# One row-scale step for the last row block, K-tile order in the first up group, and another stage order in a 2048 x 1024 decoder block

## Chip, cores and metric

The kernel runs on one core of a Trainium2 chip. The metric is device time in microseconds (us), the median of several executions; less is better. Before the change it is 2471.93 us (three runs, 2469.47 to 2472.9).

## What is computed

One decoder block on x, 2048 rows (S) by 1024 columns (D), everything in float32:

```
n  = rms_norm(x, w1)
m  = concat(gated_deltanet(n), retention(n))     # 4 heads of 128 each
h  = x + m @ w_out                               # 1024 x 1024
n2 = h * rsqrt(mean(h*h, -1) + 1e-6) * w2        # the second norm
u  = causal_dwconv3(n2 @ w_up)                   # two halves: gate and value
y  = rms_norm(h + (silu(u_gate) * u_value) @ w_down, w3)
```

The mixers (gated deltanet and retention) work in chunks with a state that is carried from chunk to chunk. The up projection makes 2 x 2816 columns.

## The kernel before, in words

**Arithmetic.** Each fp32 product is three TensorE (PE) matmuls: both operands are split into a rounded part (hi) and a rest (lo), and hi·hi, hi·lo, lo·hi are added in one bank of PSUM (mm3, lines 118 to 120). The split itself is two instructions: ACT copies the hi part (line 1045 for the output projection, 1101 for up's x and weights), and DVE subtracts it to get the lo part (1046, 1102). On top of that the three large projections (w_out, up, down) use a scheme of seven products in place of eight: seven sums of sub-blocks are formed on DVE (lines 1121 for x, 1151 for weights), then split, then multiplied, and the seven results are added up with the right signs (1017 for w_out, 1183 for up).

**Stages.** The rows are four blocks of 512 (b = 0 to 3). A string, ORDER (line 46), names the stages of all blocks in the order in which the program is written: 2b0 is the first base stage of block 2, 3W5 product 5 of block 3's output projection, 3N its second norm. The base stages (`gdn_base`) solve the triangular systems of the deltanet on POOL, as a long chain of small instructions (lines 771 and 773). A scheduler then places the instructions of the neighbouring stages on each engine, and the numbers of buffers in BUFS bound how far ahead it may go. After the mixers of all blocks follow `mlp_up` (22 column groups, each for two halves q of the rows) and `mlp_down`.

**The second norm (W_items).** When the last product of a row tile t has been added, `done(t)` stores the tile (hd), squares and sums it on ACT (1029), forms mean plus eps on DVE (1030, 128x1), takes the power -0.5 on POOL (1031, 128x1) and scales the tile in place on ACT (1032, 128x1024, tile Cw). Each block has four tiles. `norm2` then transposes the scaled tiles on PE (line 1080, bank nps) and writes them to DRAM (n2d), from where `mlp_up` reads them as xr.

**The border between mixers and up.** Half q = 0 of up needs blocks 0 and 1 only, so the first up groups run while block 3's output projection (products W1, W2, W6, W7, W5, W4, W3) ends. Four steps prepare them: `load_w` fetches a group's weights into wur, forms their sums and splits them (tile wu); `prep_x` does the same to the rows (xr, sums st, tiles x, for kt = 0 to 3). Their DMAs stand in SyncE's queue (SP) behind fences, given as FW (first weights) and F0 to F3 (the rows of kt = 0 to 3): each is an index, counted from the end, in the list of weight loads of block 3's output projection. `group(q, g, ...)` multiplies. Two groups, those in `outer`, run K-tile by K-tile over seven banks at once; all others run one product after another, each over its four K-tiles, with the bank of p1 used again for product 2 and that of p5 for product 3 (lines 1202 to 1211; ACT copies p1 out on 1203 and 1205).

Of the kernel before, what the change touches and what calls it, by code (L numbers as in the profile page):

```python
# [10 lines left out]
AF = mybir.ActivationFunctionType  # L11
ALU = mybir.AluOpType
# [12 lines left out]
NACC = 6  # L25
NWU = 9
NWV = 5
FW = -6
F0 = -7
F1 = -2  # L30
F2 = -1
F3 = -3
NU = 3
NPB = 7
NPM = 4
# [3 lines left out]
NXR = 7  # L39
FD = 4  # L40
NFRESH = 2
BUFS = {"n1": 8, "ykq": 14, "kv": 6, "NT": 13, "AT": 6, "o": 9, "n2s": 21, "xk": 2, "og": 4, "co": 7, 
        "Cw": 10, "wx": 1, "wsq": 6, "pr": 2, "pt": 3, "pv": 2, "ca": 8, "D": 9, "rk": 13, "rq": 9, 
        "rv": 25, "Ar": 4, "xs": 4, "sx": 4, "Cb": 9, "Nb": 14, "rot": 1, "rrow": 1}

ORDER = ("0pro 0v0 0k0 0dec 0a0 0q0 0a1 0a3 0a2 0h1 0b0 0h0 0L0 0Q0 0r00 0b1 0Q1 0r01 0r02 0kq 0r03 0L1 0h3 "
# [7 lines left out]
P = 128  # L54
S = 2048
D = 1024
KT = D // P
TB = 512
NB = S // TB
NT = TB // P  # L60
# [3 lines left out]
NP = NF // 2  # L64
EPS = 1e-6
# [8 lines left out]
def unit(pool, tag, shape, dt=F32, **kw):  # L74

    n = int(np.prod(shape[1:]))
    t = pool.tile([P, U1], dt, tag=tag, name=tag, **kw)[:, :n]
    if len(shape) == 3:
        t = t.rearrange("p (a b) -> p a b", a=shape[1])
    elif len(shape) == 4:  # L80
        t = t.rearrange("p (a b c) -> p a b c", a=shape[1], b=shape[2])
    return t
# [93 lines left out]
def prep_v(tc, pool, marks, w, k, nm, kept, drp, caps):  # L176

    nc = tc.nc
    POOL = nc.gpsimd
    r = [unit(pool, "pr", [P, 2, TB], bufs=caps[0]) for j in range(2)]  # L180
    for j in range(2):
        chained(tc, marks, r[j].rearrange("p a n -> p (a n)"), w[k, :, 2 * j * TB:2 * (j + 1) * TB])
    q = [r[j // 2][:, j % 2] for j in range(4)]
    tt = [unit(pool, "pt", [P, 2, TB], bufs=caps[1]) for j in range(2)]
    t1, t2, t3, t4 = (tt[j // 2][:, j % 2] for j in range(4))
    for d, a, b_ in ((t1, q[1], q[0]), (t3, q[3], q[1]), (t2, q[3], t1), (t4, q[2], t2)):
        POOL.tensor_tensor(d, a, b_, op=ALU.subtract)
    for i, src in ((1, q[0]), (2, q[2]), (3, q[3]), (5, t1), (7, t3), (6, t2), (4, t4)):
        v = split_v(nc, unit(pool, "pv", [P, 2, TB], F32R, bufs=caps[2]), src)
        kept[i, k] = drp.tile([P, 2, TB], F32, name=f"{nm}{i}_{k}", tag=f"{nm}{i}_{k}", bufs=1)  # L190
        nc.sync.dma_start(kept[i, k], v.bitcast(F32))
# [52 lines left out]
def mixers(ctx, tc, base, base_used, marks, drp, mm3, gamma, mhalf, n1w, n2w, gcw, gv127, epsr, gnw, n2d, hd,  # L244
           x, xT, w_kq, w_v, w_g, w_i, w_rk, w_r0, w_r, w_o, rows, masks, rot):
    nc = tc.nc
    PE, ACT, DVE, POOL = nc.tensor, nc.scalar, nc.vector, nc.gpsimd
# [96 lines left out]
    def kept_v(kept, i, k):  # L344
        v = unit(ap_, "wv", [P, 2, TB], F32R, bufs=NWV)
        chained(tc, marks, v.bitcast(F32), kept[i, k])
        return v

    def prep(k, which):
        def f(_):  # L350
            w, nm, kept = ((w_i, "wi", wic), (w_o, "wo", wvc))[which]
            prep_v(tc, ap_, marks, w, k, nm, kept, drp, (BUFS["pr"], BUFS["pt"], BUFS["pv"]))
        return f
# [12 lines left out]
    def al(tag, shape, dt=F32):  # L366
        return unit(ap_, tag, shape, dt, **({"bufs": BUFS[tag]} if tag in BUFS else {}))

# [6 lines left out]
    def bank(nm):  # L375
        return psb.tile([P, 512], F32, tag="bk", name=nm)

    def mbank(nm):
        return psm.tile([P, 512], F32, tag="mx", name=nm)
# [7 lines left out]
    def small(nm, n=16, bufs=2):  # L387
        if nm not in ring:
            ring[nm] = [pc(bufs, n), 0, bufs]
        e = ring[nm]  # L390
        e[1] += 1
        return e[0][:, e[1] % e[2]]
# [621 lines left out]
    def W_items(b):  # L1014
        C = {}
        ss = small("hss", 16)
        add = lambda o, a, b_: DVE.tensor_tensor(o, a, b_, op=ALU.add)

        def addx(c, src, t, dh):
            xr = al("wx", [P, TB])  # L1020
            r0 = b * TB + t * P
            marks["x", b, t, dh] = nc.sync.dma_start(xr, x[r0:r0 + P, dh * TB:(dh + 1) * TB])
            add(c, src, xr)

        def done(t):
            c = C[t]
            nc.sync.dma_start(hd[b][t * P:(t + 1) * P, :], c)
            sq = al("wsq", [P, D])
            ACT.activation(sq, c, AF.Square, accum_out=ss[:, t:t + 1])
            DVE.tensor_scalar(ss[:, t:t + 1], ss[:, t:t + 1], 1.0 / D, EPS, op0=ALU.mult, op1=ALU.add)  # L1030
            POOL.tensor_tensor(ss[:, 8 + t:9 + t], ss[:, t:t + 1], mhalf[:, :1], op=ALU.pow)
            ACT.activation(c, c, AF.Copy, scale=ss[:, 8 + t:9 + t])

        def product(i):
            def f(_):
                vs = [kept_v(wvc, i, k) for k in range(NH)]
                if b == NB - 1:
                    marks.setdefault("wo", marks["wl"][-16:]).extend(marks["vl"][-NH:])
                for m in range(2):
                    if i == 1:  # L1040
                        for t in (m, 2 + m):
                            C[t] = al("Cw", [P, D])
                    r = sts[b]["co"][i][:, :, m * P:(m + 1) * P]
                    u = unit(ap_, "wu2", [P, 2, NH, P], F32R, bufs=NU)
                    ACT.activation(u[:, 0], r, AF.Copy)
                    DVE.tensor_tensor(u[:, 1], r, u[:, 0].bitcast(F32), op=ALU.subtract)
                    ps = bank("wo")
                    mm3(ps, [(u[:, 0, k], u[:, 1, k], vs[k][:, 0], vs[k][:, 1]) for k in range(NH)])
                    c11, c12 = C[m][:, :TB], C[m][:, TB:]
                    c21, c22 = C[2 + m][:, :TB], C[2 + m][:, TB:]  # L1050
                    if i == 1:
                        ACT.activation(c12, ps, AF.Copy)
                        addx(c11, ps, m, 0)
                    elif i == 2:
                        add(c11, ps, c11)
                    elif i == 6:
                        add(c12, ps, c12)
                    elif i == 7:
                        add(c21, ps, c12)
                    elif i == 5:  # L1060
                        add(c22, ps, c21)
                        add(c12, ps, c12)
                        for c, t, dh in ((c21, 2 + m, 0), (c22, 2 + m, 1), (c12, m, 1)):
                            addx(c, c, t, dh)
                    elif i == 3:
                        add(c12, ps, c12)
                        done(m)
                    else:
                        add(c21, ps, c21)
                        done(2 + m)  # L1070
            return f

        def norm2(_):
            for kk in range(4):
                ns = al("n2s", [P, 2, TB])
                for i in range(2):
                    k = 2 * kk + i
                    ps = mbank("nps")
                    for m in range(NT):
                        PE.transpose(ps[:, m * P:(m + 1) * P], C[m][:, k * P:(k + 1) * P], ident)  # L1080
                    ACT.activation(ns[:, i], ps, AF.Copy, scale=n2w[:, k:k + 1])
                marks["n", b, kk] = nc.scalar.dma_start(n2d[b, kk].rearrange("k p t -> p k t"), ns)
        return {f"W{i}": [(None, None, product(i))] for i in ORD_DN} | {"N": [(None, None, norm2)]}

    sts = [dict() for _ in range(NB)]
    items = {b: A_items(b, sts[b]) | W_items(b) for b in range(NB)}
    items["load"], items["parts"] = load_chunk, load_parts
    return items
# [3 lines left out]
def mlp_up(ctx, tc, marks, drp, mm3, mcw, mhalo, n2d, wud, aud, w_u):  # L1092
    nc = tc.nc
    PE, ACT, DVE, POOL = nc.tensor, nc.scalar, nc.vector, nc.gpsimd
# [159 lines left out]

    gs = [(0, g) for g in range(2 * NP)]
    gs += [(1, g) for g in (*range(NFRESH, NP + 1), *range(NFRESH), *range(NP + 1, 2 * NP))]
    outer = [gs[2 * NP - 1], gs[2 * NP]]
    marks["f1"] = [g // 2 for q, g in gs[2 * NP::2]]
    st = {}
    fence = [marks["wo"][j].ins for j in (FW, F0, F1, F2, F3)]  # L1260
    with tc.issue_after(fence[0]):
# [209 lines left out]
```

## Time and profile before

| | us |
|---|---|
| median of three runs | 2471.93 |
| the profiled execution, its time | 2470.93 |
| its span, first to last instruction | 2469.1 |
| PE busy | 2408.9 |
| DVE busy | 1642.7 |
| ACT busy | 1010.1 |
| POOL busy | 549.2 |
| mean granted PE clock (of 1) | 0.994 |

The span is made of mixers up to about 1166 us, the border up to about 1221 us, up, and down to the end. In the profile's rows, L118 is line 118 of the kernel, PE and PEld are matmuls and weight loads of TensorE, PEclk is the clock that TensorE was granted; in a timeline each row has start, duration, engine, line, output<-input, and in brackets the idle time ahead of it and what ended it; in the waits, the total, the count and the longest.

### The profile page before, as it was taken

What the parts mean: (1) busy time and instruction counts of PE and PEld (TensorE: products, weight loads), DVE (VectorE), ACT (ScalarE), POOL (GpSimd) and SP (SyncE); (2) the same over time, 40 slices, a digit from 0 to 9 for tenths busy, and PEclk for the clock granted to TensorE, in tenths of its full rate; (3) what the DMA queues carried; (4) which work ended last, traced back from release to release, by engine and by line L of the source; (5) the groups of instructions that cost most, each with busy time, mean ns of one, the idle gap of its engine ahead of it and who ended that gap; (6) DMA issues with size and microseconds to landing.
All of it is one profiled execution on the core that took longest, in us unless ns stands there. A gap on an engine that the chain in (4) does not pass through costs nothing.

```text
span 2469.1 us, 35787 instructions
## 1 busy us (share of the span) xinstructions
PE 2408.9 (98%) x12508; PEld 2022.4 (82%) x12508; DVE 1642.7 (67%) x3260; ACT 1010.1 (41%) x2125; POOL 549.2 (22%) x865
## 2 busy tenths in 40 slices
PE   9999899999999999999899999999999999999998
PEld 7877788888888888787588888888888888888887
DVE  5886966355754646436989889896575567555673
ACT  5554634444522543325554344442232225333341
POOL 1385214701083104530211000000000001422030
PEclk9999999999999999999999999999999999999999
DMA  5887866674565565546698788787646879864782
GB/s 214 289 302 273 311 226 229 237 246 167 203 235 189 193 231 187 195 177 233 220 337 301 288 312 294 282 298 248 226 155 245 284 242 285 265 211 141 237 257 95
DMA packets 281572, 590.05 MB, mean 239 GB/s; under 512 B 40560, under 2 KB 120880, under 8 KB 281392
## 3 DMA queue, kind: packets, MB, share of 16 engines
q1 hardware_dynamic: 264528, 573.40, 66.2%
q10 hardware_dynamic: 16864, 14.37, 1.8%
q8 instruction: 98, 1.61, 0.3%
q14 instruction: 82, 0.67, 0.1%
HBM read 395.42 MB, written 192.25 MB: 238 GB/s over the span
## 4 chain that ended last, share of the span: by engine, by line
PE 81%; POOL 8%; DVE 4%; DMA 3%; issue 2%; ACT 1%; SPq 0%; ACTq 0%; POOLq 0%; DVEq 0%
PE p L118 11%; PE p L120 11%; PE p L119 11%; PE d L120 6%; PE d L119 6%; PE d L118 6%; PE tok L561 4%; PE tok L563 4%; PE tok L562 4%; POOL pers L773 3%; POOL pers L771 3%; PE chm L118 2%; PE chm L119 2%; PE chm L120 2%; PE wo L120 1%
## 5 line engine op out<-in xcount | busy, mean ns | idle before, releaser
L119 PE MATMUL p<-x,wu 128*128 128x512 f32 x1176 | 459.3, 391 | 3.3 <-DVE x L1102 3.3
L118 PE MATMUL p<-x,wu 128*128 128x512 f32 x1176 | 454.6, 391 | 7.1 <-ACT x L1101 6.7
L120 PE MATMUL p<-x,wu 128*128 128x512 f32 x1176 | 452.3, 390 | 0.0
L561 PE MATMUL tok<-wc,n 128*128 128x512 f32 (+2 forms) x768 | 277.7, 364 | 5.8 <-ACT n L449 5.5
L562 PE MATMUL tok<-wc,n 128*128 128x512 f32 (+2 forms) x768 | 276.4, 361 | 0.0
L563 PE MATMUL tok<-wc,n 128*128 128x512 f32 (+2 forms) x768 | 275.3, 362 | 0.0
L118 PEld LDWEIGHTS p<-x,wu 128*128 128x128 f32 x1176 | 221.0, 188 | 56.9 <-ACT x L1101 8.7
L119 PEld LDWEIGHTS p<-x,wu 128*128 128x128 f32 x1176 | 221.4, 188 | 51.4 <-DVE x L1102 6.2
L120 PEld LDWEIGHTS p<-x,wu 128*128 128x128 f32 x1176 | 221.4, 188 | 46.0 <-DVE wu L1102 0.2
L1225 DVE SCALAR_TENSOR_TENSOR acc<-uc,base,acc 128x1022 f32<-128x1022 f32 (+1 forms) x176 | 221.0, 1279 | 39.0 <-ACT acc L1222 38.9
L1183 DVE TENSOR_TENSOR uc<-p,uc 128x512 f32<-128x512 f32 x224 | 153.4, 688 | 122.5 <-PE p L120 122.0
L118 PE MATMUL d<-v,uu 128*128 128x512 f32 x448 | 174.3, 389 | 0.0
L119 PE MATMUL d<-v,uu 128*128 128x512 f32 x448 | 174.3, 389 | 0.0
L120 PE MATMUL d<-v,uu 128*128 128x512 f32 x448 | 174.3, 389 | 0.0
L561 PEld LDWEIGHTS tok<-wc,n 128*128 128x128 f32 x768 | 146.8, 191 | 26.4 <-ACT n L449 5.5
L220 POOL TENSOR_TENSOR vt<-vr 128x512 f32<-128x512 f32 x33 | 51.6, 1574 | 516.5 <-DVE acc L1238 421.7
L563 PEld LDWEIGHTS tok<-wc,n 128*128 128x128 f32 x768 | 146.7, 191 | 20.0
L562 PEld LDWEIGHTS tok<-wc,n 128*128 128x128 f32 x768 | 146.8, 191 | 19.3
L119 PE MATMUL chm<-n,wc 128*128 128x512 f32 x384 | 151.2, 394 | 0.0
L120 PE MATMUL chm<-n,wc 128*128 128x512 f32 x384 | 151.2, 394 | 0.0
L118 PE MATMUL chm<-n,wc 128*128 128x512 f32 x384 | 151.1, 393 | 0.0
L771 POOL TENSOR_TENSOR pers<-Nb,pers 128x248 f32<-128x248 f32 (+30 forms) x248 | 119.5, 482 | 69.5 <-DMA Nb<-z 53.5
(256 smaller groups left out, 4804.8 us busy)
## 6 DMA issues: line engine op xcount, KB each, us to landing
wu<-wu SPq DMA_DIRECT2D x280, 512.0 KB, 5.9
wc<-wd SPq DMA_DIRECT2D x166, 512.0 KB, 5.6
wv<-wo SPq DMA_DIRECT2D x112, 512.0 KB, 6.4
wd<-wc SPq DMA_DIRECT2D x60, 512.0 KB, 4.9
ur<-au SPq DMA_DIRECT2D x56, 512.0 KB, 5.0
wur<-in_w_u SPq DMA_DIRECT2D x48, 512.0 KB, 6.3
au<-st SPq DMA_DIRECT2D x88, 256.0 KB, 4.1
vr<-in_w_d SPq DMA_DIRECT2D x77, 256.0 KB, 5.3
```

The lines of the kernel that those rows point to most:

```text
L118: PE.matmul(ps, ah, bh, start=(first and i == 0), stop=False, skip_group_check=chk)
L119: PE.matmul(ps, ah, bl, start=False, stop=False, skip_group_check=chk)
L120: PE.matmul(ps, al, bh, start=False, stop=(i == n - 1), skip_group_check=chk)
L220: POOL.tensor_tensor(tt[:, j], a, b_, op=ALU.subtract)
L561: PE.matmul(ps, ah, wh, start=(k == 0), stop=False)
L562: PE.matmul(ps, ah, wl, start=False, stop=False)
L563: PE.matmul(ps, al_, wh, start=False, stop=(k == KT - 1))
L771: POOL.tensor_tensor(tm[:, :, :n], Nb[:, j:j + 1, j + 1:].to_broadcast([P, 8, n]), X[:, :, j:j + 1].to_broadcast([P, 8, n]), op=ALU.mult)
L773: POOL.tensor_tensor(X[:, :, j + 1:], X[:, :, j + 1:], tm[:, :, :n], op=ALU.add)
L1183: add = lambda o, ps, a: DVE.tensor_tensor(o, ps, a, op=ALU.add)
L1225: DVE.scalar_tensor_tensor(acc[:, t:], u[:, :T2 - t], w, acc[:, t:], op0=ALU.mult, op1=ALU.add)
```

## The change

Five edits:

1. **Last block's row scales.** The steps of lines 1030 to 1032 become a function `rms(ts)`. Blocks 0 to 2 call it per tile, as before. Block 3 calls it once, at the head of `norm2`, for all four tiles: one DVE instruction and one POOL instruction of 128x4, then four ACT scales.
2. **First up group.** `outer` takes in the very first group: seven banks, K-tile outermost. It has two more DVE additions than the form before, and one ACT copy less.
3. **Fences.** The first weights' load moves six places ahead in the list of loads (from behind W4's third load to behind W5's first); the rows' loads move by one to three places.
4. **ORDER** differs from block 1's state steps on (from "1r12 2k0 1G1a" to the end of block 3's).
5. **BUFS**: other numbers of buffers for sixteen tile names.

```
-FW = -6
-F0 = -7
-F1 = -2
-F2 = -1
-F3 = -3
+FW = -12
+F0 = -6
+F1 = -5
+F2 = -4
+F3 = -4
...
-         "1r10 1r11 1h3 1G0a 1r12 2k0 1G1a 2v0 1r13 1W1 1G0b 1W2 2dec 2a0 1G1b 2a2 2a1 2b0 1W6 1W7 1W5 2a3 "
+         "1r10 1r11 1h3 1G0a 1r12 1G1a 2k0 2v0 1W1 1G0b 1W2 2dec 1r13 1G1b 2a0 2a1 1W6 2a2 1W7 1W5 2a3 2q0 "
...
+        def rms(ts):
+            a, e = ts[0], ts[-1] + 1
+            DVE.tensor_scalar(ss[:, a:e], ss[:, a:e], 1.0 / D, EPS, op0=ALU.mult, op1=ALU.add)
+            POOL.tensor_tensor(ss[:, 8 + a:8 + e], ss[:, a:e], mhalf[:, :e - a], op=ALU.pow)
+            for t in ts:
+                ACT.activation(C[t], C[t], AF.Copy, scale=ss[:, 8 + t:9 + t])
+
         def done(t):
...
-            DVE.tensor_scalar(ss[:, t:t + 1], ss[:, t:t + 1], 1.0 / D, EPS, op0=ALU.mult, op1=ALU.add)
-            POOL.tensor_tensor(ss[:, 8 + t:9 + t], ss[:, t:t + 1], mhalf[:, :1], op=ALU.pow)
-            ACT.activation(c, c, AF.Copy, scale=ss[:, 8 + t:9 + t])
+            if b < NB - 1:
+                rms((t,))
...
         def norm2(_):
+            if b == NB - 1:
+                rms(range(NT))
...
-    outer = [gs[2 * NP - 1], gs[2 * NP]]
+    outer = [gs[0], gs[2 * NP - 1], gs[2 * NP]]
```

In the rows below, lines of the changed kernel have moved: 1030, 1031, 1032 and 1029 are now 1027, 1028, 1030 and 1036; lines from 1045 on are 6 to 8 higher (1046 is 1052, 1102 is 1110, 1151 is 1159, 1183 is 1191, 1225 is 1233). A number behind a tile's name tells one buffer from another. The number of TensorE matmuls is the same, and their order is the same up to the 588th us of the span before, again in block 3's mixers (1043 to 1166 us), and from the 1365th us on.

**First place: DVE at the border**, around the lo parts for W5's and W4's operands (wu with a number, from co) and the first up group's weights (wu without a number, from wur and the sums st). Before:

```order
L1046 TENSOR_TENSOR wu_11932<-co,wu_11932 128x512
L1017 TENSOR_TENSOR Cw<-wo,Cw 128x512 x4
L1017 TENSOR_TENSOR Cw<-Cw,wx 128x512
L1046 TENSOR_TENSOR wu_11955<-co,wu_11955 128x512
L1046 TENSOR_TENSOR wu_11986<-co,wu_11986 128x512
L1102 TENSOR_TENSOR x_0_12140<-xr,x_0_12140 128x512
L1102 TENSOR_TENSOR wu<-wur,wu 128x512 x2
L1151 TENSOR_TENSOR st<-wur 128x512 x2
```

Now, at the same place on DVE:

```order
L1052 TENSOR_TENSOR wu_11932<-co,wu_11932 128x512
L1110 TENSOR_TENSOR wu<-wur,wu 128x512 x2
L1159 TENSOR_TENSOR st<-wur 128x512 x2
L1159 TENSOR_TENSOR st<-st,wur 128x512
L1159 TENSOR_TENSOR st<-wur,st 128x512
L1110 TENSOR_TENSOR wu<-st,wu 128x512 x3
L1110 TENSOR_TENSOR wu<-wur,wu 128x512
L1017 TENSOR_TENSOR Cw<-wo,Cw 128x512 x2
L1110 TENSOR_TENSOR wu<-st,wu 128x512
L1017 TENSOR_TENSOR Cw<-wo,Cw 128x512 x2
L1052 TENSOR_TENSOR wu_11952<-co,wu_11952 128x512
L1052 TENSOR_TENSOR wu_11980<-co,wu_11980 128x512
```

Eleven instructions for the first group's weights, which stood among the rows' splits, now stand ahead of W5's four additions and of the next operand's lo part.

**Second place: ACT, and DVE, at the last block's row scales** (Cw are the four tiles, pers_116 the scales, x with numbers and wu are up's operands, uc and acc its results). ACT before:

```order
L1101 ACTIVATE x_1_12188<-st 128x512
L1203 ACTIVATE uc<-p_12293 128x512
L1032 ACTIVATE Cw<-Cw,pers_116 128x1024
L1101 ACTIVATE x_2_12215<-st 128x512
L1205 ACTIVATE uc<-p_12293 128x512
L1101 ACTIVATE x_3_12245<-st 128x512
```

ACT now:

```order
L1211 ACTIVATE uc<-p_12445 128x512
L1213 ACTIVATE uc<-p_12445 128x512
L1036 ACTIVATE wsq,pers_116<-Cw 128x1024
L1230 ACTIVATE acc<-uc,base 128x1024 x2
L1030 ACTIVATE Cw<-Cw,pers_116 128x1024 x4
L1109 ACTIVATE wu<-st 128x512 x2
```

DVE now, around the one instruction (L1027) that the joint power on POOL waits for:

```order
L1191 TENSOR_TENSOR uc<-p_12293,uc 128x512
L1159 TENSOR_TENSOR st<-st,wur 128x512
L1027 TENSOR_SCALAR pers_116<-pers_116 128x4
L1191 TENSOR_TENSOR uc<-p_12500,uc 128x512
L1159 TENSOR_TENSOR st<-wur,st 128x512
L1233 SCALAR_TENSOR_TENSOR acc<-uc,base,acc 128x1023
L1191 TENSOR_TENSOR uc<-p_12514,uc 128x512
L1233 SCALAR_TENSOR_TENSOR acc<-uc,base,acc 128x1023
```

The first scale no longer stands among the copies of x on ACT. All four now stand behind the last copy of x, behind the second group's first copies out of PSUM and behind two instructions of the first group's convolution (L1230).

**Third place: POOL at the end of block 2's first base stage** (the pairs L771 and L773 are the last steps of its chain of 31, L701 and L768 small steps of block 2's deltanet, L908 a step of block 1's retention queries rq, L1028 a row scale of block 1). Before:

```order
L771 TENSOR_TENSOR pers_1665<-Nb,pers_1665 128x8x3
L773 TENSOR_TENSOR pers_1665<-pers_1665 128x8x3
L908 TENSOR_TENSOR rq<-rq,pers_401 128x128
L771 TENSOR_TENSOR pers_1665<-Nb,pers_1665 128x8x2
L908 TENSOR_TENSOR rq<-rq,pers_401 128x128
L773 TENSOR_TENSOR pers_1665<-pers_1665 128x8x2
L908 TENSOR_TENSOR rq<-rq,pers_401 128x128
L771 TENSOR_TENSOR pers_1665<-Nb,pers_1665 128x8
L908 TENSOR_TENSOR rq<-rq,pers_401 128x128
L773 TENSOR_TENSOR pers_1665<-pers_1665 128x8
L908 TENSOR_TENSOR rq<-rq,pers_401 128x128 x4
```

Now:

```order
L771 TENSOR_TENSOR pers_1665<-Nb,pers_1665 128x8x2
L773 TENSOR_TENSOR pers_1665<-pers_1665 128x8x2
L771 TENSOR_TENSOR pers_1665<-Nb,pers_1665 128x8
L701 TENSOR_TENSOR pers_628<-pers_401,base 128x4
L773 TENSOR_TENSOR pers_1665<-pers_1665 128x8
L779 MEMSET AT 128x512
L768 COPY pers_1665<-base 128x256
L908 TENSOR_TENSOR rq<-rq,pers_401 128x128 x8
L1028 TENSOR_TENSOR pers_116<-pers_116,base 128x1
```

The eight steps of rq, which stood between the last pairs of the chain, now stand together behind the whole chain; the step L701 of block 2's fourth head, which stood ahead of the pair 128x8x13, now stands in the chain's last pair.

More of the change, by code (lines that the diff above doesn't have):

```diff
@@ L41 @@
 NFRESH = 2
-BUFS = {"n1": 8, "ykq": 14, "kv": 6, "NT": 13, "AT": 6, "o": 9, "n2s": 21, "xk": 2, "og": 4, "co": 7,
-        "Cw": 10, "wx": 1, "wsq": 6, "pr": 2, "pt": 3, "pv": 2, "ca": 8, "D": 9, "rk": 13, "rq": 9,
-        "rv": 25, "Ar": 4, "xs": 4, "sx": 4, "Cb": 9, "Nb": 14, "rot": 1, "rrow": 1}
+BUFS = {"n1": 8, "ykq": 15, "kv": 4, "NT": 13, "AT": 10, "o": 7, "n2s": 23, "xk": 2, "og": 11, "co": 7,
+        "Cw": 11, "wx": 1, "wsq": 5, "pr": 2, "pt": 3, "pv": 2, "ca": 10, "D": 14, "rk": 6, "rq": 7,
+        "rv": 31, "Ar": 11, "xs": 4, "sx": 4, "Cb": 5, "Nb": 23, "rot": 1, "rrow": 3}
 ORDER = ("0pro 0v0 0k0 0dec 0a0 0q0 0a1 0a3 0a2 0h1 0b0 0h0 0L0 0Q0 0r00 0b1 0Q1 0r01 0r02 0kq 0r03 0L1 0h3 "
```

6 rows, old and new, of the table ORDER are left out of this document.

## Prediction

> **What bounds the kernel now.** I read the page first, then the stretches, the waits of TensorE (PE), and at last the timeline around the largest wait.
>
> The page's first rows, and the matmul group with the most idle time, are these:
>
> ```profile
> span 2469.1 us, 35787 instructions
> PE 2408.9 (98%) x12508; PEld 2022.4 (82%) x12508; DVE 1642.7 (67%) x3260; ACT 1010.1 (41%) x2125; POOL 549.2 (22%) x865
> L118 PE MATMUL p<-x,wu 128*128 128x512 f32 x1176 | 454.6, 391 | 7.1 <-ACT x L1101 6.7
> ```
>
> PE is the bound, and a change that leaves its matmuls alone can win no more than its 2469.1 − 2408.9 = 60.2 us of idle time, and what it loses to a lower clock. The stretches tell where that idle time lies (columns: PE, PEld, DVE, ACT, POOL busy, granted clock, DMA share, GB/s):
>
> ```profile
> 588.00:1043.00 455.00, 443.79 (x2573) 379.88 (x2573) 255.27 (x751) 182.15 (x515) 146.37 (x277) 1.00 0.58 202
> 1043.00:1166.00 123.00, 117.05 (x838) 99.86 (x837) 60.20 (x184) 50.21 (x135) 32.66 (x72) 0.99 0.55 200
> 1166.00:1300.00 134.00, 121.60 (x522) 94.87 (x521) 118.85 (x181) 69.42 (x111) 27.30 (x13) 0.97 0.77 282
> 1300.00:2469.10 1169.10, 1162.04 (x5126) 961.74 (x5124) 827.73 (x1142) 416.08 (x615) 120.05 (x106) 1.00 0.72 246
> ```
>
> PE is idle for 11.2 us in the mixers of blocks 1 to 3, 5.9 us in block 3's end (where its order stays), 12.4 us at the border to up, and 7.1 us in all the rest. So what the change can move lies in two places: the border, where DVE is the busy one (118.85 of 134 us), and the mixers from 588 us on. The waits name the pieces:
>
> ```profile
> PE p L118 <- ACT x L1101: 6.7, 4, 5.5
> PE p L119 <- DVE x L1102: 3.3, 6, 1.2
> PE kqtr L688 <- DVE ca L670: 2.7, 1, 2.7
> PE mxt L584 <- DVE Cb L583: 2.4, 2, 1.9
> PE rtr L959 <- POOL rq L908: 2.2, 1, 2.2
> PE rkk L965 <- ACT ykq L960: 1.9, 2, 1.6
> ```
>
> The largest one is a single wait of 5.5 us for an ACT copy of x. ACT's timeline says why it was late, and POOL's why ACT was:
>
> ```profile
> 1199.20 0.58 ACT L1203 ACTIVATE uc<-p 128x512 f32<-128x512 f32 x1
> 1206.31 1.15 ACT L1032 ACTIVATE Cw<-Cw,pers 128x1024 f32<-128x1024 f32 x1 [6.52 <-POOL pers L1031]
> 1207.36 0.61 ACT L1101 ACTIVATE x<-st 128x512 fp32r<-128x512 f32 x1
> ```
>
> ```profile
> 1190.29 15.99 POOL L1031 TENSOR_TENSOR pers<-pers,base 128x1 f32<-128x1 f32 x1 [47.12 <-DVE pers L1030]
> 1223.38 1.45 POOL L1031 TENSOR_TENSOR pers<-pers,base 128x1 f32<-128x1 f32 x2 [17.10 <-DVE pers L1030]
> 1259.40 2.39 POOL L1230 COPY base<-uc 128x2 f32<-128x2 f32 x1 [9.51 <-DVE uc L1183]
> ```
>
> A power over 128x1 took 15.99 us at 1190.29, while two others took 1.45 us together. DVE's timeline shows what ran meanwhile, and when it stopped:
>
> ```profile
> 1205.16 0.70 DVE L1121 TENSOR_TENSOR st<-xr,st 128x512 f32<-128x512 f32 x1
> 1208.01 0.69 DVE L1102 TENSOR_TENSOR x<-st,x 128x512 fp32r<-128x512 f32 x1 [2.15 <-ACT x L1101]
> 1218.34 0.68 DVE L1102 TENSOR_TENSOR x<-st,x 128x512 fp32r<-128x512 f32 x1
> 1261.65 0.69 DVE L1183 TENSOR_TENSOR uc<-p,uc 128x512 f32<-128x512 f32 x1
> ```
>
> From the power's start DVE worked without a break, on instructions that read both inputs from SBUF, up to 1205.86; the power ended at 1206.28, as soon as DVE ran dry, and DVE ran dry since ACT, which works in order, stood at the scale that needs the power. So each waited for the other until DVE had nothing left. The small POOL copy at 1259.40 ended at 1261.79, when DVE had begun L1183, which reads PSUM: that form lets POOL in. The Trainium skill, SBUF — State Buffer, "Who interferes with whom", says that DVE with two SBUF inputs and a POOL instruction that reads SBUF share a lock which is held for one whole instruction. The trace agrees on who shuts out whom, but not on the length: here POOL lost some 26 instructions in a row, 15.99 us against 0.70.
>
> PE then paid twice:
>
> ```profile
> 1202.14 0.39 PE L118 MATMUL p<-x,wu 128*128 128x512 f32 x1
> 1208.03 0.80 PE L118 MATMUL p<-x,wu 128*128 128x512 f32 x1 [5.50 <-ACT x L1101]
> 1212.66 0.42 PE L118 MATMUL p<-x,wu 128*128 128x512 f32 x1
> 1206.00:1208.00 2.00, 0.00 (x0) 0.00 (x0) 0.00 (x0) 1.67 (x2) 0.28 (x1) 0.50 0.64 230
> 1214.00:1216.00 2.00, 2.00 (x11) 1.64 (x10) 2.00 (x5) 0.47 (x1) 0.00 (x0) 1.00 0.63 246
> ```
>
> After the wait the clock stood at 0.50, and ten matmuls took 1212.66 − 1208.03 = 4.63 us; at the later pace (the eleven in the 2 us from 1214, listed 0.227 us apart) they take 2.3. So the clock cost 2.3 us and the wait 5.5.
>
> **The change, part by part.** *Joint row scales and the new place of the first scale.* They remove the power from the stretch in which DVE works on x: three DVE instructions of 128x1 and three on POOL go, and the four scales stand behind all copies of x. The 5.5 us wait goes, with its 2.3 us of clock. What is late next is DVE itself, since it is nearly always busy there.
>
> *First weights earlier, first group K-tile by K-tile.* DVE sat idle ahead of W5's additions, waiting for PE:
>
> ```profile
> 1164.76 1.37 DVE L1017 TENSOR_TENSOR Cw<-wo,Cw 128x512 f32<-128x512 f32 x2 [2.87 <-PE wo L120]
> 1170.20 2.48 DVE L1017 TENSOR_TENSOR Cw<-wo,Cw 128x512 f32<-128x512 f32 x4 [2.87 <-PE wo L120]
> 1173.20 1.29 DVE L1046 TENSOR_TENSOR wu<-co,wu 128x512 fp32r<-128x512 f32 x2
> wur<-in_w_u SPq DMA_DIRECT2D x48, 512.0 KB, 6.3
> ```
>
> Now ten of the eleven weight instructions start where it went idle, 1170.20 − 2.87 = 1167.33. One of 128x512 takes a step of 0.60 us (1170.20 to 1173.20 is five). They end at 1173.3, and behind them DVE has, by the new order, 64 such instructions up to the last split of x: 1173.3 + 64 × 0.60 = 1211.7. Before, that split ended at 1218.34 + 0.68 = 1219.0. DVE is 7.3 us ahead. Their weights must have landed by 1167; the fence lets the load go six weight loads earlier, which by my reading of the queue is some 6 us earlier than 1160.8, and with 6.3 us to land it is there at about 1161.
>
> The cost: W4's operand (the 1.29 us row at 1173.20) is now split behind ten weight instructions, and PE, which waited 1.28 us for it before, waits until about 1176.5, some 4.4 us in all. That is on PE but not on the end, since PE would wait for DVE's x splits later anyway. It is weighed by two prices. By the row at 1208.03, a wait of 5.50 us halves the clock and costs 2.3 us more, which would be hidden in the same slack. The Trainium skill, TensorE: Matmul & The Clock Gate, Part 1, says that an idle window of about 3.4 us halves the clock and as much work restores it; the trace's 0.50 agrees, though here the low clock lasted from 1206 to 1212. By that rule the new wait may slow PE until about 1183; the border's gain would then be 8 if the slack covers it, and 5 to 6 if not.
>
> The sum at the border, from PE: its idle time there is 12.4, with 2.3 of clock 14.7. After the change remain the 4.4 and some 2 us of single waits for DVE, so 8.3 is won; by DVE's lead it is 7.3. I take 8, with ends of 3 (only the idle time of DVE that is filled, 2.87) and 9.5.
>
> The seven banks cost two more DVE additions, 1.2 us, in a stretch where PE works on the second group. Then PE has sixteen transposes (nps) in a row, which need all four scales. By the rows' order the joint power starts at about 1224.5, and four scales at 1.15 us (the 1206.31 row) end at about 1231; PE comes to them at about 1233. That is a slack of 2 us.
>
> *Stage order and buffers.* PE's instructions are the same, so only its waits can change. In the new order block 2's base chain runs ahead of the rq steps and starts earlier, so the 2.2 (rtr) and the 1.6 us (rkk, behind an ACT scale) at 719 to 729 us should go: −3.8. Block 3's kqtr keeps its 2.7 us wait and has less work beside it (about 2 us in place of 5), +0 to +3; the recurrences' waits such as mxt's 1.9 may move either way. Between −5 and +5 I take −2, nearest to the two rows that go, less half of what may come.
>
> Sum: 2470.93 − 8 − 2 = 2461 us for the profiled execution; the median of the runs is 1.0 above that execution, so 2462.
>
> **The rivals.**
>
> *The border gives back what it wins.* PE waits for W4's operand, the clock falls, the slack doesn't cover it, and only DVE's filled idle time of about 3 us is won; the mixers give nothing: 2472 − 3 = 2469. For it: DVE is busy 118.85 of 134 us and sets the pace with or without the power. Against it: 64 × 0.60 us from 1173.3 ends well before 1219.0. Chance 0.20.
>
> *The mixers lose.* A new wait in blocks 2 or 3 as long as the largest one now (2.7), with a drop of the clock (2.3), costs 5; the border wins 8: 2472 − 8 + 5 = 2469. Chance 0.12.
>
> *Slower: the joint power is shut out again.* It has the same engine and the same neighbour, DVE, but now all four scales hang on it, PE's sixteen transposes hang on them, and the second group's matmuls stand behind those. If it takes 15.99 us again, the scales end 15 us later, the slack is 2, PE stands 13 us and loses 2.3 of clock: 2472 − 10 + 15 = 2477. It turns slower than before from a power of some 10 us on, and by over 0.2% only at the full length. For it: L1230's 2.39 us copies, which show that POOL still loses three or four DVE instructions in a row there. Against it: right behind the instruction that it waits for, DVE has an addition from PSUM (L1191), one sum from SBUF, and then the convolution (L1233) and PSUM in turn; and the power at 1223.38 ran in 1.45 for two among the same kinds. Chance 0.08.
>
> By the rule of the Trainium skill (SBUF — State Buffer, the same section) a loss is one instruction only, so this last case could not happen; the row of 15.99 us speaks against that, and I keep it.
>
> **How the numbers follow.** The forecast as summed has a chance of 0.60, the rivals 0.20, 0.12 and 0.08. A difference of 0.2%, 5 us, is about what a measurement of this kernel can tell from no change. The two cases at 2469 end on either side of 2467; of their 0.32 I put 0.10 with faster and 0.22 with the same. So faster 0.70, same 0.22, slower 0.08. The range: low, both terms at their better ends, 2472 − 9.5 − 5 = 2457, less 2 for the scatter of runs, 2455; high, the two middle rivals with as much scatter, 2469 + 2, and some of what lies beyond, 2474.
>
> **What would show it right or wrong.** In the profile after: the longest power on POOL is below 3 us (right) or over 10 (the slower rival); the wait of p for the ACT copy of x is gone from the top of PE's waits; the clock is 1.00 in all 2 us pieces after the last products of w_out; the last x split comes 6 to 8 us earlier relative to W5's additions; the waits rtr and rkk at 719 to 729 are gone. It would be wrong if PE's idle time in the up stretch behind the border, which is none now, became several us, or if the sum of the waits before 1043 us rose above the 11.2 us of before.

## The result

The changed kernel takes 2452.55 us (median) against 2470.7 before, in the same stretch of measurements; the ratio is 0.9927, 95% interval 0.9908 to 0.9946. In a second measurement (run e5 below) it was 2453.95 against 2473.35, ratio 0.9922, 0.9908 to 0.9935. The forecast was 2462, 10 us less than before, with a range of 2455 to 2474. The measured time lies below that range: the direction was right, the size not. Of the four runs of the changed kernel one was disturbed (2970.63 us) and is left out of the ratio; the other three lie between 2451.56 and 2452.65.

The page of the changed kernel begins so:

```profile
span 2449.8 us, 35748 instructions
PE 2400.1 (98%) x12508; PEld 2017.1 (82%) x12508; DVE 1642.0 (67%) x3259; ACT 1008.6 (41%) x2124; POOL 525.4 (21%) x862
```

Two things got smaller, not one. PE's idle time went from 60.2 to 49.7 us, but its busy time fell too, from 2408.9 to 2400.1, for the same 12508 matmuls: less of it was spent at a low clock, and the mean granted clock rose from 0.994 to 0.998. The stretches (PE, PEld, DVE, ACT, POOL busy, clock, DMA share, GB/s) are cut at the same times as before, though the work now reaches each cut earlier:

```profile
588.00:1043.00 455.00, 449.59 (x2609) 385.74 (x2608) 256.28 (x765) 184.19 (x511) 153.68 (x295) 1.00 0.58 207
1166.00:1300.00 134.00, 130.17 (x574) 104.24 (x575) 125.45 (x185) 74.70 (x117) 7.11 (x12) 1.00 0.80 298
```

In the mixers PE is idle for 5.4 us in place of 11.2; in the border's stretch for 3.8 in place of 12.4, and the clock there is 1.00 in place of 0.97. The 3.8 flatters the change, since the border's first waits now fall ahead of the cut at 1166 us (PE's idle time from 1043 to 1166 us rose from 5.9 to 9.1). Between the same matmuls, the 6750th and the 8000th, the idle time fell from 14.3 to 8.5 us. PE's waits that were named before read now:

```profile
PE wo L118 <- ACT wu L1051: 3.2, 2, 1.7
PE p L1199 <- DVE x L1110: 2.0, 4, 0.8
PE wo L120 <- DVE wu L1052: 2.0, 3, 1.4
PE p L1198 <- ACT x L1109: 1.3, 2, 1.1
PE rtr L959 <- POOL rq L908: 1.1, 1, 1.1
PE rkk L965 <- ACT ykq L960: 0.4, 1, 0.4
PE kqtr L688 <- ACT ykq L684: 0.3, 1, 0.3
```

The wait of 5.5 us for an ACT copy of x is gone (the largest of that kind is 1.1), and so is kqtr's 2.7 us for DVE. The joint power, its scales and the transposes behind them:

```profile
1216.17 1.01 POOL L1028 TENSOR_TENSOR pers<-pers,base 128x4 f32<-128x4 f32 x1
1217.61 4.26 ACT L1030 ACTIVATE Cw<-Cw,pers 128x1024 f32<-128x1024 f32 x4
1222.53 1.91 PE L1088 MATMUL nps<-base,Cw 128*128 128x128 f32 x16
```

The power takes 1.01 us for four columns, the four scales end at 1221.87, and PE takes up the sixteen transposes at 1222.53 without a wait: just in time, with 0.7 us to spare.

DVE at the border, from the first weights on, and at the last split of x:

```profile
1154.06 1.37 DVE L1017 TENSOR_TENSOR Cw<-wo,Cw 128x512 f32<-128x512 f32 x2 [2.87 <-PE wo L120]
1155.34 1.28 DVE L1052 TENSOR_TENSOR wu<-co,wu 128x512 fp32r<-128x512 f32 x2
1156.55 1.29 DVE L1110 TENSOR_TENSOR wu<-wur,wu 128x512 fp32r<-128x512 f32 x2
1165.75 1.28 DVE L1052 TENSOR_TENSOR wu<-co,wu 128x512 fp32r<-128x512 f32 x2
1200.66 0.68 DVE L1110 TENSOR_TENSOR x<-st,x 128x512 fp32r<-128x512 f32 x1
```

The second idle time of 2.87 us, ahead of W5's additions, is filled with the first group's weights. The last split of x ends at 1201.3 in place of 1219.0, that is 17.7 us earlier. PE's 6750th matmul, at which the border begins, starts 10.7 us earlier (1.9 of these lie ahead of the mixers, where the order is as before), so 7.0 were won at the border; the forecast was 7.3.

### The profile page after: what moved, and what is told of

It reads as the page before. It is cut to its first block, busy times and chain, and to the rows that moved or that the text cites. A ratio compares the mean times of both kernels' runs of the same rounds, so it can differ in the third digit from the quotient of the medians.

```text
span 2449.8 us, 35748 instructions
## 1 busy us (share of the span) xinstructions
PE 2400.1 (98%) x12508; PEld 2017.1 (82%) x12508; DVE 1642.0 (67%) x3259; ACT 1008.6 (41%) x2124; POOL 525.4 (21%) x862
## 4 chain that ended last, share of the span: by engine, by line
PE 88%; DVE 4%; POOL 3%; DMA 2%; issue 1%; ACT 1%; SPq 0%; ACTq 0%; POOLq 0%; DVEq 0%
PE p L118 11%; PE p L120 11%; PE p L119 11%; PE d L119 6%; PE d L118 6%; PE d L120 6%; PE tok L561 5%; PE tok L563 5%; PE tok L562 5%; PE chm L119 3%; PE chm L118 3%; PE chm L120 3%; PE wo L120 2%; PE wo L118 2%; PE wo L119 2%
## 5 line engine op out<-in xcount | busy, mean ns | idle before, releaser
L119 PE MATMUL p<-x,wu 128*128 128x512 f32 x1148 | 446.6, 389 | 0.0
L118 PE MATMUL p<-x,wu 128*128 128x512 f32 x1148 | 442.7, 389 | 0.0
L120 PE MATMUL p<-x,wu 128*128 128x512 f32 x1148 | 440.1, 389 | 0.0
L118 PEld LDWEIGHTS p<-x,wu 128*128 128x128 f32 x1148 | 215.6, 188 | 45.4 <-ACT n2s L1089 0.4
L120 PEld LDWEIGHTS p<-x,wu 128*128 128x128 f32 x1148 | 215.6, 188 | 44.9 <-DVE wu L1110 0.4
L119 PEld LDWEIGHTS p<-x,wu 128*128 128x128 f32 x1148 | 215.5, 188 | 44.6
L771 POOL TENSOR_TENSOR pers<-Nb,pers 128x248 f32<-128x248 f32 (+30 forms) x248 | 118.7, 479 | 57.2 <-DMA Nb<-z 41.3
```

Of the source, the lines that this page charges most:

```text
L118: PE.matmul(ps, ah, bh, start=(first and i == 0), stop=False, skip_group_check=chk)
L119: PE.matmul(ps, ah, bl, start=False, stop=False, skip_group_check=chk)
L120: PE.matmul(ps, al, bh, start=False, stop=(i == n - 1), skip_group_check=chk)
L771: POOL.tensor_tensor(tm[:, :, :n], Nb[:, j:j + 1, j + 1:].to_broadcast([P, 8, n]), X[:, :, j:j + 1].to_broadcast([P, 8, n]), op=ALU.mult)
```

## The experiments

For each profiled run the matmul records of PE were counted; since every kernel here issues the same number of them, the start of the n-th record can be compared between runs. "Mixers" is the time from the 3250th to the 6000th record (554 to 1037 us in the kernel before), "border" from the 6750th to the 8000th (1140 to 1440 us). "Waits" is PE's idle time in the mixers. "Low clock" is what PE lost there to its clock: between the 3250th and the 8000th record the clock is either full or 0.50, the latter for 3.4 or 6.8 us at a time, and half of that time counts as lost. The mixers less these two columns are 469.4 to 470.3 us in all 17 profiled executions, so waits and clock together account for the differences. The stretch up to the 3250th record has the same order of instructions in all of them, and scatters from 545.8 to 550.6 us without any relation to the edit, so a single profiled span can't be read closer than about 2 us. From the 8000th record on all take 1021.9 us, but 1022.3 in e6.

| run | against before | ratio (95%) | mixers | waits | low clock | border |
|---|---|---|---|---|---|---|
| before | | | 483.2 | 11.2 | 1.7 | 300.0 |
| after | −18.2 | 0.9927 (0.9908 to 0.9946) | 475.1 | 5.4 | 0.0 | 291.4 |
| e1 joint scales alone | −4.5 | 0.9984 (0.9975 to 0.9993) | 484.4 | 9.6 | 5.1 | 297.2 |
| e2 all border edits | −5.4 | 0.9976 (0.9967 to 0.9985) | 486.9 | 11.8 | 5.1 | 293.3 |
| e3 order and buffers | −8.6 | 0.9964 (0.9950 to 0.9978) | 474.6 | 5.1 | 0.0 | 303.1 |
| e4 after, scales per tile | −16.6 | 0.9933 (0.9921 to 0.9946) | 476.6 | 5.1 | 1.7 | 294.8 |
| e5 after, again | −19.4 | 0.9922 (0.9908 to 0.9935) | 476.3 | 5.1 | 1.7 | 291.4 |
| e6 after, no K-tile order | −17.8 | 0.9924 (0.9911 to 0.9936) | 474.9 | 5.3 | 0.0 | 292.0 |
| e7 after, old fences | −15.3 | 0.9930 (0.9918 to 0.9943) | 475.0 | 5.2 | 0.0 | 294.3 |
| e8 a copy from PSUM | −1.7 | 0.9993 (0.9985 to 1.0002) | 485.5 | 10.4 | 5.1 | 298.1 |
| e9 buffers alone | −1.0 | 0.9998 (0.9989 to 1.0007) | 486.7 | 11.7 | 5.1 | 301.6 |
| e10 order, block 2's start | −2.9 | 0.9992 (0.9983 to 1.0000) | 482.4 | 9.2 | 3.4 | 300.5 |
| e11 order, block 3 | −4.7 | 0.9981 (0.9972 to 0.9990) | 483.3 | 9.7 | 3.4 | 301.6 |
| e12 K-tile order and fences | −3.8 | 0.9985 (0.9976 to 0.9994) | 486.8 | 11.8 | 5.1 | 297.1 |
| e13 order, middle | −1.0 | 1.0000 (0.9991 to 1.0008) | 486.6 | 13.3 | 3.4 | 302.1 |
| e14 order, both ends | −10.0 | 0.9957 (0.9943 to 0.9971) | 478.7 | 5.9 | 3.4 | 300.0 |
| e15 order alone | −8.9 | 0.9960 (0.9947 to 0.9972) | 474.9 | 5.2 | 0.0 | 302.0 |

"Against before" is the difference of the medians on the same chip, in us.

### The power that stands: e1, e4, e8, e12

The theory was that the power on POOL and DVE's work on x wait for each other, and that ending this frees PE; the rival, that DVE sets the pace of the border with or without it. **e1** is the kernel before with `rms` and its two calls, nothing else:

```
+            if b < NB - 1:
+                rms((t,))
...
+            if b == NB - 1:
+                rms(range(NT))
```

> The kernel before with the joint row scales alone. Theory (the power on POOL and the DVE work on x wait for each other): no power is longer than 3 us, PE's 5.5 us wait for the ACT copy of x and its slow clock go, and the time falls by 5 to 8 us. Rival (DVE sets the pace of the border with or without the power): PE's waits there move to the DVE splits of x, and the time falls by 3 us or less.

The power took 1.01 us (at 1230.80), and the 5.5 us wait went, but only 4.5 us of time (by the interval, 1.7 to 6.2); at the border 2.8 of its 300. The waits for DVE's splits of x are seven now:

```profile
PE p L119 <- DVE x L1110: 3.9, 7, 1.3
```

That is little more than the 3.3 us of before, so these waits did not take the place of the long one. PE's waits at the border fell by 3.9 us (14.3 to 10.4). What did not go is the low clock: it stood at 0.50 for 3.4 us each from 1156.1 and from 1197.0 us on, behind short waits (1.67 us, and 1.25 us with smaller ones ahead), and cost 3.2 us of PE's work at the border, where the kernel before lost 2.3. So the theory was right on the wait and wrong on the clock, and the rival was wrong on where PE's waits go; the 4.5 us lie between what the two expected. **e8** ends the stall without moving a scale. Behind each of the last block's powers stands one more DVE instruction, a copy out of PSUM that nobody reads:

```
             POOL.tensor_tensor(ss[:, 8 + t:9 + t], ss[:, t:t + 1], mhalf[:, :1], op=ALU.pow)
+            if b == NB - 1:
+                DVE.tensor_copy(sq[:, :TB], ps)
```

> The kernel before with one more instruction on DVE behind each of the last block's L1030: a copy of 128x512 from PSUM that nobody reads. Theory (POOL's power is let in when DVE reads PSUM, or runs dry): the first power ends within 1 us in place of 16, PE's 5.5 us wait goes, and the time falls by 2 to 5 us though DVE has four instructions more. Rival (the power is slow for a reason on POOL, or DVE's count of work decides): it stays near 16 us, and the time is as before or up to 3 us longer.

POOL and DVE in e8:

```profile
1191.90 0.56 POOL L1031 TENSOR_TENSOR pers<-pers,base 128x1 f32<-128x1 f32 x1 [47.05 <-DVE pers L1030]
```

```profile
1191.67 0.15 DVE L1030 TENSOR_SCALAR pers<-pers 128x1 f32<-128x1 f32 x1
1191.73 0.68 DVE L1033 COPY wsq<-wo 128x512 f32<-128x512 f32 x1
1192.33 0.69 DVE L1104 TENSOR_TENSOR x<-st,x 128x512 fp32r<-128x512 f32 x1
```

The same power takes 0.56 us in place of 15.99, because it starts while DVE reads PSUM. That shows the cause of the long power. The time fell by 1.7 us only, which can't be told from none (the interval goes from 3.7 less to 0.5 more). PE's waits at the border fell by 3.9 us as in e1, but the clock cost 4.7 us there, at other places, and DVE has four copies more to run, 0.60 us each. So the wait of 5.5 us with its slow clock was 7.8 us long, and the two runs without it are 1.7 and 4.5 us faster.

**e4** is the changed kernel with `rms((t,))` for all blocks, **e12** the kernel before with the new fences and `outer`, so both have the scales per tile.

> The changed kernel with the last block's row scales per tile again. Theory: a power of over 10 us stands on POOL among the DVE work on x, PE waits for an ACT copy of x, and the time rises by 5 to 8 us over the changed kernel (to 2458 to 2461). Rival (DVE sets the pace): it rises by 2 us or less.

> The kernel before with the K-tile order and the fences, but the row scales per tile. Theory (DVE sets the pace of the border, and the early weights give it work while it was idle): the border is 3 to 5 us shorter than before, though a power on POOL may still be long. Rival (the power decides): no gain, and PE waits 5 us or more for ACT.

Here the power was neither 16 us nor 0.6. In e4 it started at 1193.30 and took 3.35 us; in e12 it took 5.15. POOL of e12, and DVE of e12 at its end:

```profile
1207.36 5.15 POOL L1031 TENSOR_TENSOR pers<-pers,base 128x1 f32<-128x1 f32 x1 [59.84 <-DVE pers L1030]
```

```profile
1211.41 0.68 DVE L1102 TENSOR_TENSOR x<-st,x 128x512 fp32r<-128x512 f32 x1
1212.01 0.68 DVE L1183 TENSOR_TENSOR uc<-p,uc 128x512 f32<-128x512 f32 x1
```

The power ends at 1212.51, half a microsecond after DVE's first instruction that reads PSUM had begun. In e4 it is the same: the end at 1196.65, and this DVE row:

```profile
1196.15 0.68 DVE L1017 TENSOR_TENSOR Cw<-wo,Cw 128x512 f32<-128x512 f32 x1
```

So the power lasts up to the next instruction of DVE that reads PSUM, or up to the time when DVE runs dry, and its length is an accident of the order. e12 also shows the mutual wait at its smaller price: PE waits 3.79 us for ACT once, and the border is still 3 to 4 us shorter than before. The time of e4 is 16.6 less than before, e5's, on another chip, 19.4: the joint scales are worth about 3 us in the changed kernel (3.4 at the border; the two runs' intervals overlap), not the 5 to 8 that the theory wanted.

### The other edits of the border: e2, e5, e6, e7

**e2** is the kernel before with the new fences, `rms` and `outer`; **e5** the changed kernel again; **e6** and **e7** are the changed kernel with one line each put back:

```
-    outer = [gs[0], gs[2 * NP - 1], gs[2 * NP]]
+    outer = [gs[2 * NP - 1], gs[2 * NP]]
```

and, in e7, FW, F0, F1, F2, F3 = −6, −7, −2, −1, −3.

> The kernel before with all of the border's edits (joint scales, first up group K-tile by K-tile, fences), old stage order and buffers. Theory (border and mixers add up, the border being worth 9.4 us in the two traces): 8 to 10 us less than before, and the mixers up to 1043 us as before. Rival (the border's gain needs the new stage order): 5 us or less.

> The changed kernel once more, as the measure for its variants on the same chip. Both theories: 2451 to 2455 us, and the matmul stream 8 us ahead of the kernel before after the mixers and 17 to 20 us ahead at the 8000th matmul.

> The changed kernel without the K-tile order in the first up group. Theory (DVE sets the pace of the border and the K-tile order lets PE work on the first K-tiles of all seven products while DVE splits the rest): 3 to 6 us slower than the changed kernel. Rival (the early weights do it, PE's order is of no account as DVE ends at the same time): within 1 us.

> The changed kernel with the fences of before: the first weights are loaded six places later. Theory (the early weights fill DVE's idle time ahead of W5's additions): DVE sits idle twice for 2.9 us there again, and the time rises by 2 to 5 us. Rival (the K-tile order does it): within 1 us.

The old order's border without any edit takes 300.0 to 303.1 us (before, e3, e9, e10, e11, e13, e14, e15; mean 301.4). With the joint scales it is 297.2, with K-tile order and fences 297.1, with all three 293.3: 4.1, 4.3 and 8.1 us, which add up. In waits and clock, the unedited borders have 14.8 us of waits on average and lose 3.2 to the low clock while PE works, the changed kernel 8.5 and none; e2 and e4 to e7 lose nothing to the clock there either. In the changed kernel, 291.4 in all, taking away the joint scales costs 3.4, the fences 2.9, the K-tile order 0.7. e6's rival came nearer: the K-tile order is of little account (median 1.6 us, the intervals of e5 and e6 cover each other). In e7 DVE is idle again ahead of W5's additions:

```profile
1161.74 2.48 DVE L1017 TENSOR_TENSOR Cw<-wo,Cw 128x512 f32<-128x512 f32 x4 [2.87 <-PE wo L120]
```

and its 2.87 us are as much as the fences are worth there. e2's time (−5.4) came out below what was expected from the border (8 to 10). Its border did get 6.8 to 8.1 us shorter; its mixers took 486.9 in the profiled execution, and the runs' medians can't be split further. The interval of e2 reaches 8.2 us. With e3 (below) it makes 14.0, where the whole change gives 18 to 19; given the intervals, it is neither shown nor excluded that border and order simply add up.

### The stage order: e3, e9, e10, e11, e13, e14, e15

**e3** is the kernel before with the new ORDER and BUFS; **e9** has only the new BUFS, **e15** only the new ORDER. **e10**, **e11** and **e13** have the new string in one of three pieces (cut where both strings have named the same stages so far), **e14** in the first and the last:

```
e10: ... 1r12 1G1a 2k0 2v0 1W1 1G0b 1W2 2dec 1r13 1G1b 2a0 2a1 1W6 2a2 1W7 1W5 2a3 2q0 2h1 2b0 | as before
e13: as before up to 2h1 | 2b1 1W4 ... 2r03 2r12 2r13 2h3 2G1a 3k0 2G1b 2G0a | as before
e11: as before up to 2G0a | 3dec 3a1 2W1 3v0 2G0b 2W2 3a0 2W6 2W7 3q0 2W5 3h1 3a3 3h0 3b0 ...
```

> The kernel before with the new stage order and buffers alone. Theory: PE's matmul stream is 8 us ahead by the end of block 3's mixers, with the waits kqtr, rtr and rkk gone or halved, the border's 5.5 us wait stays, and the time falls by 7 to 10 us. Rival (the difference in the mixers is a matter of the execution that was profiled): 2 us or less.

> The kernel before with the new buffer numbers alone; no instruction changes its place. Theory (the mixers' gain is the stage order's): within 2 us of the kernel before, with the waits rtr, rkk and kqtr as they were. Rival (buffers that came free too late were behind the waits): 4 us less or more.

> The kernel before with the whole new stage order, old buffers. Theory (buffers are of no account): 8 to 10 us less, as with the new buffers. Rival (the order needs them): 6 us or less.

The order alone does it: e15 is as fast as e3, and the buffers alone change nothing that can be told from none. With the old order the mixers take 485.6 us (mean of before, e1, e2, e8, e9, e12), with the new one 475.3 (after, e3, e4, e5, e6, e7, e15).

> The kernel before with the new stage order up to block 2's stage 2h1 only (block 1's end and block 2's start), old buffers. Theory (POOL's chain of block 2's first base stage runs earlier and no longer cuts into rq, and the ACT scale behind it no longer waits): the 2 to 3 us wait rtr and the wait rkk go, with the slow clock at 720 to 730 us, 3 to 5 us less. Rival (these waits are made up for later): 1 us less or none.

> The kernel before with the new stage order from block 3's stage 3dec on only, old buffers. Theory (DVE no longer stands at the transposes that wait for block 3's base chain, so the kqtr wait of 2.1 to 3.0 us goes): 3 to 5 us less in the mixers. Rival, as the prediction had it (kqtr keeps its wait): no change, or slower.

> The kernel before with the new stage order only between block 2's stage 2h1 and block 3's stage 3dec (block 2's state steps), old buffers. Theory (the three pieces of the new order add up, and 4 to 5 us of the mixers' 10 are still without a piece): 3 to 5 us less in the mixers. Rival (the rest comes only where the pieces meet): 1 us or less.

> The kernel before with the new stage order up to 2h1 and from 3dec on, but the old one between them, old buffers. Theory (the pieces add up): 5 to 6 us less in the mixers. Rival (what block 2's start wins is lost at block 3's kqtr unless block 3's order moves too): 8 us or more, with neither rtr nor kqtr above 1 us.

e10 takes away most of rtr (0.7 us are left) and all of rkk at block 2's start, where POOL's chain now ends before the rq steps are due, but kqtr in block 3 grows. Its 2.9 us lie between theory and rival, and its interval holds both. This is the place in the kernel before, then in e10 (DVE and PE):

```profile
1011.22 0.71 DVE L784 STREAM_TRANSPOSE NT<-AT 128x512 f32<-128x512 f32 x1 [7.59 <-DMA AT<-z]
1014.98 0.68 DVE L670 TENSOR_TENSOR ca<-chm,rrow 128x512 f32<-128x512 f32 x1
1015.81 0.63 PE L688 MATMUL kqtr<-base,ykq 128*128 128x128 f32 x4 [2.71 <-DVE ca L670]
```

```profile
1007.61 0.71 DVE L784 STREAM_TRANSPOSE NT<-AT 128x512 f32<-128x512 f32 x1 [8.62 <-DMA AT<-z]
1011.38 0.68 DVE L670 TENSOR_TENSOR ca<-chm,rrow 128x512 f32<-128x512 f32 x1
```

```profile
1012.21 0.63 PE L688 MATMUL kqtr<-base,ykq 128*128 128x128 f32 x4 [3.73 <-DVE ca L670]
```

In e10 DVE stands for 8.62 us at a transpose that waits for the end of POOL's chain and its DMA, and the instruction that kqtr needs stands behind it. With the new order of block 3 that chain starts earlier: at 943.91 us in the changed kernel and at 952.92 in e11, against 964.32 in the kernel before. DVE of the changed kernel:

```profile
991.19 0.71 DVE L784 STREAM_TRANSPOSE NT<-AT 128x512 f32<-128x512 f32 x1 [5.49 <-DMA AT<-z]
991.83 0.65 DVE L670 TENSOR_TENSOR ca<-chm,rrow 128x512 f32<-128x512 f32 x1
996.69 0.69 DVE L670 TENSOR_TENSOR ca<-chm,rrow 128x512 f32<-128x512 f32 x1
1001.35 0.69 DVE L670 TENSOR_TENSOR ca<-chm,rrow 128x512 f32<-128x512 f32 x1
```

DVE still stands at a transpose, but this time 10 us ahead of the last L670 (4 us before), and kqtr finds that one done. e14 has both, −10.0, and neither wait is above 0.8 us, as its rival had it; e13, the middle, gives nothing, as its own rival had it. The sum of e10 and e11, −7.6, and e14 agree within their intervals, so that the pieces meet in some other way isn't shown.

## Why the prediction was wrong

**The failed step** is the one on stage order and buffers: "Between −5 and +5 I take −2". The mixers gave 10 us (485.6 to 475.3; 8.0 between the two profiled executions of before and after), and the order alone 8.6 and 8.9 by the medians of e3 and e15. Two things were wrong in it.

The first is the sentence "Block 3's kqtr keeps its 2.7 us wait and has less work beside it". The prediction counts kqtr's wait by the work that PE has beside it, not by what stands in DVE's queue ahead of the L670: the transpose, at which DVE was idle for 7.59 us. With the chain ahead by 11 to 20 us, the wait went: it is 2.1 to 3.7 us in the eight profiled executions with the old block 3, and 0 to 0.4 in the nine others.

The second is a term that the sum did not have: what the clock does behind waits shorter than 3 us. In the profiled execution of before, the clock read 1.00 behind the waits at 719 and 729 us, so these were priced at their length. But the same execution lost 1.7 us a little later, which the stretch of 455 us, rounded to 1.00, does not show:

```profile
720.00:730.00 10.00, 8.44 (x43) 6.67 (x42) 4.26 (x11) 4.45 (x7) 5.86 (x12) 1.00 0.71 235
870.00:880.00 10.00, 7.65 (x51) 6.85 (x50) 7.16 (x28) 9.27 (x31) 2.43 (x3) 0.83 0.08 27
```

In the other runs with the old order it fell at both places. e1 (columns as above, the clock is the third from the end):

```profile
710.00:720.00 10.00, 7.61 (x37) 6.17 (x36) 2.22 (x10) 0.73 (x2) 8.59 (x29) 0.96 0.29 99
720.00:730.00 10.00, 9.64 (x40) 7.37 (x39) 4.29 (x13) 4.45 (x7) 5.76 (x12) 0.87 0.72 220
870.00:880.00 10.00, 7.66 (x50) 6.39 (x50) 6.60 (x27) 8.47 (x30) 3.02 (x3) 0.81 0.08 27
880.00:890.00 10.00, 10.00 (x43) 8.48 (x42) 7.35 (x25) 8.45 (x31) 0.00 (x0) 0.85 0.47 152
```

Ten us at 0.87 are 1.3 us lost, and the four rows together 5.1. e6, with the new order, at the same places:

```profile
720.00:730.00 10.00, 10.00 (x51) 8.38 (x50) 2.20 (x5) 5.58 (x8) 7.91 (x13) 1.00 0.93 346
870.00:880.00 10.00, 8.94 (x52) 7.34 (x52) 7.07 (x23) 9.26 (x31) 1.01 (x1) 1.00 0.17 54
```

Between e1 and e6 the mixers' time without PE's waits differs by 474.8 − 469.7 = 5.1 us, the same as these rows.

The other runs agree. Between 719 and 736 us, behind rtr or rkk, the clock fell in seven of the eight profiled executions with the old start of block 2, and in none of the nine with the new one. Between 870 and 887 us, behind a wait of mxt of 1.7 to 1.9 us with smaller ones beside it, it fell in all nine with the old middle piece, and in two of the eight with the new one. (In e8, e10 and e13 it fell behind kqtr too.) Of the 10 us, 5.9 are waits (11.1 to 5.2, means of the runs above), of which rtr, rkk and kqtr make 5.4, and 4.0 are clock (4.5 to 0.5). The waits of rtr and rkk, forecast to go with 3.8 us, gave 2.9 on these means; kqtr, forecast to cost 0 to 3, gave 2.5; and the clock stood at nothing.

One reading ahead of the sum is incomplete, without harm to it: the four idle times that are listed make 36.6 of the 60.2 us, and "all the rest" leaves out the first 588 us, which hold the other 23.6 and which the change does not touch.

**The border** was forecast at 8 and is 8.6 between the two profiled executions, 10 against the mean of the unedited borders. The size held (14.3 to 8.5 us of waits, 2.3 to none of clock), but not what the single edits give. The prediction has the joint scales take away 5.5 us of wait and 2.3 of clock; alone they took 4 us of wait and none of the clock, which fell at other places (e1, e8). By the border's time the joint scales are worth 3 to 4 us, the early weights some 3. That DVE sets the pace of the border and the change gives only 3 us there was the first rival; its price was wrong, since the early weights give DVE work in the time in which it was idle, and the joint scales come on top. Against W5's additions, by which the prediction wanted to measure the last split of x, it comes 10.2 us earlier and not 6 to 8, as these additions themselves stand behind the weights now.

**W4's operand** was to cost 4.4 us of wait with a clock at half behind it. PE took it up at 1166.49, which is 1177.2 on the old scale (10.7 us were won ahead of it), about the 1176.5 of the working; but PE had work in between, and waited twice, for 1.57 and 1.42 us (3.0 in all), with the clock at 1.00. The Trainium skill, TensorE: Matmul & The Clock Gate, Part 1, puts the limit at about 3.4 us of idle time; both waits lie below, so the row agrees here. It does not agree in the mixers, where a wait of 2.40 us, next to a PE that was busy before and after it, was enough in e1.

**The joint power** behind PE's transposes, the slower rival, did not come: 1.01 us, and 0.7 us of slack in place of the 2 that I had worked out. In e2 the same power took 2.59 us, so it is not always this cheap.

**The mixers' other waits** went as written: rtr from 2.2 to 1.1 us and rkk's 1.6 at 729 to none, 2.7 of the 3.8 that were named.

## What to carry to other kernels

Do not price a stall by its length alone: of 7.8 us of wait and slow clock, two ways of taking away the stall gave 1.7 and 4.5 us, because some wait came back at the next operands and the clock fell behind shorter waits. Where an in-order engine stands at an instruction that waits for a long chain, read which later instructions stand behind it and when they are due; moving that chain's start by 11 us or more took away a wait of 2 to 3 us that I had counted as fixed. And read the clock behind each wait in more than one execution before pricing it at its length.

## What the runs showed of the hardware

A POOL instruction of half a microsecond that reads SBUF can be held off for as long as DVE runs instruction after instruction with both inputs in SBUF: 15.99 us in before and 16.59 in e3 (one of the two in all eight runs with an unedited border), 5.15 in e12, 3.35 in e4, 0.56 in e8. In the three shorter ones it ended 0.5 to 0.7 us after the start of a DVE instruction that reads PSUM, in the two long ones when DVE ran dry. (Each of these instructions that read PSUM also has at most one input in SBUF; no run tells the one from the other.) The Trainium skill, SBUF — State Buffer, "Who interferes with whom", has an exclusive lock, and whoever issues first holds it for the whole instruction while the other blocks. These runs agree on the forms that exclude each other, but the waiting POOL instruction did not get its turn between two DVE instructions. The section does not say who comes next; that a loss lasts one instruction only, as the prediction has it, was worked out from it.

Waits below 3 us lowered PE's clock in some executions and not in others. It was 0.50 for 3.4 us behind a wait of 2.40 us in e1, but stayed at 1.00 behind one of 2.41 us at the same place in e12 and of 2.20 us in before. Behind mxt's 1.66 us and three shorter waits it fell in e5, and not in the other profiled execution of the same kernel, after, with the same waits. What decides it was not tried.
